# Operand loads of the down stage moved from GpSimd's queue to ScalarE's, one by one

## The chip, the core and the metric

The kernel runs on one NeuronCore of a Trainium2 chip. A core has five engines with a queue of instructions each: TensorE (PE in the profile; its weight loads are PEld), VectorE (DVE), ScalarE (ACT), GpSimd (POOL) and SyncE (SP). They work side by side and wait for each other by semaphores. Transfers between HBM and the on-chip memory are asked for by an instruction on SP's, ACT's or POOL's queue and carried by 16 DMA engines that all three share. The metric is the device time of one execution in microseconds.

## The reference

One encoder block over 512 positions of width 2048, all in float32. Attention, its output projection and the residual come first; this case is about the last part, the feed-forward network:

```python
h = rmsnorm(x, norm_ffn[l])
x = x + (jax.nn.silu(h @ w_gate[l]) * (h @ w_up[l])) @ w_down[l]
return rmsnorm(x, norm_final)
```

`w_gate` and `w_up` are 2048 x 5632, `w_down` is 5632 x 2048. The product with `w_down` is the down stage.

## The kernel before, in words

Every float32 operand is split into a high part and a low remainder (a CAST on ACT, then a subtraction on DVE), and each product is three matmuls: high x high, high x low, low x high (lines 184 to 186, the helper `mm3`). Matrix products of the feed-forward stages go by a Strassen-like scheme with seven products for a 2 x 2 block, named "11", "s3", "s2", "12", "s1", "22" and "s4"; the combinations of weights are made on DVE (L593, L596, L598, L603), then cast on ACT (L612) and subtracted on DVE (L613). Weights come through SP's queue (L583), four transfers of 512 KB for a unit.

In the gate and up stage (`unit_gu`, 44 units) each pair of hidden tiles leaves seven combinations, high and low side by side. They are written to HBM into `combos`, 1792 KB for a pair (7 x 512 floats, 14,336 bytes, in each of 128 partitions). The first pair and the last two do not take this way: their activations go as they are to `acts_kept`, stored by SP from the tile `raw` (L703).

The down stage starts with `unit_first`: four plain units for the first pair, whose results ACT copies out of PSUM (L768, L769) into eight accumulator tiles, one of them the former `raw`. Then come 19 pairs in five chunks of 4, 4, 4, 4 and 3 (`CHUNKS`). A chunk has four units (`unit_dn`, one for each quarter of the output's columns), and each unit runs the seven products over the chunk's pairs: 24 matmuls a product with four pairs. The results of a product lie in PSUM banks (of eight, handed out in turn) and are added to the accumulators (L790 of the kernel before; L806 and L814 copy a bank to a work tile on ACT, L810 forms the sum `u2` on DVE).

`load_operands` fetches a chunk's combinations from `combos`, one transfer for a pair (L747). Seven places take them in turn: `cp0` to `cp5` and `w0`, so pair i goes to place (i - 1) % 7, the next chunk's first three pairs have places that the running chunk does not use, and the fourth has to wait until PE leaves the running chunk's first place (for the later chunks, the previous one's). That fourth pair is asked for at the chunk's start; so the first unit of chunks 1 to 4 (`apart`) runs the first four products over three pairs, and then completes each with the fourth pair, by 6 matmuls (chunk 4 has no fourth pair). Before the change all 19 loads stand on POOL's queue: chunk 0's four in `unit_first`, the next chunk's first three in unit 1, the fourth in unit 0 of its own chunk.

PE's order is as written. The other engines' lists are put in order by the scheduler, from dependencies and its own estimate of when things are ready; so a request stands where the scheduler puts it, not where the source has it. Each engine runs its list strictly in that order.

Of the kernel before, what the change touches and what calls it, by code (L numbers as in the profile page):

```python
# [10 lines left out]
F32 = mybir.dt.float32  # L11
# [18 lines left out]
CHUNKS = [range(1 + 4 * c, min(5 + 4 * c, 20)) for c in range(5)]  # L30
# [15 lines left out]
def encoder_block(ctx: ExitStack, tc: tile.TileContext, io):  # L46
    nc = tc.nc
    pe, act, dve, pool = nc.tensor, nc.scalar, nc.vector, nc.gpsimd
# [23 lines left out]
    def bank():  # L72
        return psum.tile([P, 512], F32, name="bank")
# [7 lines left out]
    def w_tile():  # L81
        return work.tile([P, 512], F32, name="wk")
# [100 lines left out]
    def mm3(out, lh, ll, rh, rl, start, stop, **kw):  # L183
        pe.matmul(out, lh, rh, start=start, stop=False, **kw)  # L184
        pe.matmul(out, lh, rl, start=False, stop=False, **kw)  # L185
        pe.matmul(out, ll, rh, start=False, stop=stop, **kw)  # L186
# [382 lines left out]
    combos = tc.dram_tile((NF // 2, P, 7, 512), F32, name="combos")  # L569
# [50 lines left out]
    def product_of(i, j, ahead=3):  # L620
        make_to(i * 7 + j + ahead)
        return made[i * 7 + j]
# [97 lines left out]
    acts, acc, ops = {}, {}, {}  # L720
# [18 lines left out]
        for j, k in enumerate(((2, 1), (3, 0), (3, 1))):  # L739
            acc[k] = w[:, 2 * j:2 * j + 2].rearrange("p a q -> p (a q)")  # L740

    def load_operands(c, some=slice(None)):
        for i in CHUNKS[c][some]:
            n = (i - 1) % 7
            t = (pools["xa"], f"cp{n}") if n < 6 else (pools["mx"], "w0")
            ops[i] = t[0].tile([P, 7, 512], F32R, name=t[1])
            pool.dma_start(ops[i].bitcast(F32), combos[i])  # L747

    def unit_first():

        places_for_acc()
        load_operands(0)
        dve.tensor_scalar_mul(nr2, r2, -1.0)
        for u in range(DN):
            wh, wl = batch()
            if u == 3:
                limit[0] = len(UNITS) * 7
                make_to(NF * 7 + 2)
            b = [bank() for _ in range(NT)]
            for f in range(2):  # L760
                ws = slice(f * 512, (f + 1) * 512)
                for t in range(NT):
                    mm3(b[t], acts[f][:, t * P:(t + 1) * P], acts[f][:, 512 + t * P:512 + (t + 1) * P],
                        wh[:, ws], wl[:, ws], start=f == 0, stop=f == 1)
                yield
            for t in range(NT):
                o = acc[u, t // 2][:, (t % 2) * 512:(t % 2 + 1) * 512]
                act.copy(o[:, :256], b[t][:, :256])  # L768
                act.activation(o[:, 256:], b[t][:, 256:], AF.Copy, scale=-1.0)  # L769

    def unit_dn(c, u):
        pairs = CHUNKS[c]
        apart = c > 0 and u == 0
        if u == 0 and c > 0:
            load_operands(c, slice(3, None))
        if u == 1 and c + 1 < len(CHUNKS):
            load_operands(c + 1, slice(0, 3))
        i0 = NF + c * DN + u
        al, be, gm = bank(), bank(), bank()
        de = bank() if apart else al  # L780
        into = {"11": al, "s3": gm, "s2": de, "12": be, "s1": de, "22": gm, "s4": de}
        s1, u2 = w_tile(), w_tile()
        r = {(h, l): acc[u, l - 1].rearrange("p (t h q) -> p t h q", t=2, h=2)[:, :, h - 1]
             for h in (1, 2) for l in (1, 2)}

        def flat(x):
            return x.rearrange("p (t q) -> p t q", t=2)

        def add(h, l, x):
            dve.tensor_add(r[h, l], flat(x), r[h, l])  # L790

        def product(i, some):
            n = PRODUCTS[i]
            wh, wl = product_of(i0, i, 3 - i if some is early else 3)
            for p in some:
                x = ops[p][:, OPERAND[n]]
                ws = slice((p - pairs[0]) * 256, (p - pairs[0] + 1) * 256)
                for t in range(2):
                    mm3(into[n][:, t * 256:(t + 1) * 256], x[:, t * P:(t + 1) * P],
                        x[:, 256 + t * P:256 + (t + 1) * P], wh[:, ws], wl[:, ws],  # L800
                        start=p == pairs[0] and t == 0 and n in ("11", "s3", "12") + ("s2",) * apart,
                        stop=p == pairs[-1], skip_group_check=True)

        def after(i):
            if i == 0:
                act.copy(s1, al)  # L806
            elif i == 1:
                add(2, 2, gm)
            elif i == 2 and apart:
                dve.tensor_add(u2, de, s1)  # L810
                add(2, 2, s1)
                add(1, 2, s1)
            elif i == 2:
                act.copy(u2, al)  # L814
            elif i == 3:
                add(1, 1, be)
                add(1, 1, s1)
            elif i == 4:
                add(2, 2, de)
                add(2, 1, u2)  # L820
            elif i == 5:
                add(2, 1, gm)
            else:
                add(1, 2, de)

        early = pairs[:3]
        if apart:
            for i in range(4):
                product(i, early)
                yield  # L830
        for i in range(7):
            product(i, pairs[3:] if apart and i < 4 else pairs)
            after(i)
            if i0 == len(UNITS) - 1 and i == 3:
                prepare_last()
            yield
        if c == len(CHUNKS) - 1:
            for t in range(2):
                add_x1(t, u)

    def add_x1(t, u):
        x1 = w_tile()
        nc.sync.dma_start(x1, x1_kept[t, u])
        y = rest[t, u] = acc[u, t // 2][:, (t % 2) * 512:(t % 2 + 1) * 512]
        for h, r in enumerate((r2, nr2)):
            s = slice(h * 256, (h + 1) * 256)
            dve.scalar_tensor_tensor(y[:, s], y[:, s], r[:, t:t + 1], x1[:, s], op0=OP.mult, op1=OP.add)
# [16 lines left out]
    def prepare_last():  # L864
        for f in range(NF - CF, NF):
            act_tile(f, late_tile())
        load_gfin()
        fetch()
        fetch()
# [106 lines left out]
    for c in range(len(CHUNKS)):  # L976
        for u in range(DN):
            drive(unit_dn(c, u))
# [75 lines left out]
```

## Time and profile before

| | |
|---|---|
| median of 3 runs | 2224.97 us (2224.67 to 2231.49) |
| profiled execution | 2224.93 us, span 2223.2 us, granted TensorE clock 0.995 |
| busy share of PE, DVE, ACT, POOL | 98%, 75%, 45%, 0% |
| loads of `combos` on POOL's queue | 17 and 2, of 1792 KB |
| loads of weights on SP's queue (`st`) | 199 of 512 KB, 3.7 us to landing (median) |
| transfers on ACT's queue | 16 of 256 KB, all before the feed-forward stages |

The page of the profile has the busy time of each engine, the span in slices, the DMA queues, the chain of work that ended last, and the costliest groups of instructions. A row of the timeline has the start in us from the span's start, the length in us, engine, line, operation, output and inputs, and in brackets how long the engine stood idle before it and what ended that. A row of the waits has who waited, for whom, us in total, how often, and the longest. In a row for one tile, three numbers with slashes are the shortest, the median and the longest.

The down stage runs from about 1750 us: `unit_first` until 1772.5, chunk 0 until about 1852, chunks 1 to 4 until about 2160.

### The profile page before, as it was taken

How to read it: one execution, taken by the hardware profiler on the slowest of the kernel's cores; microseconds unless marked ns; L12 is line 12 of the kernel's file. 1: busy time of each engine (PE TensorE's matmuls, PEld its weight loads, DVE VectorE, ACT ScalarE, POOL GpSimd, SP SyncE). 2: the span in 40 equal slices, each digit the busy share in tenths (PEclk: the TensorE clock that was granted, in tenths of full speed). 3: DMA queues.
4: the chain of work that ended last, by engine and by line, in shares of the span. 5: the costliest groups of instructions: out<-in, count | busy, mean ns of one | idle time of the engine just before them, and what ended most of it. 6: DMA issues, size and time to landing. Idle time of an engine off the chain costs nothing. (4 is left out here: it accounts for less than half of the span.)

```text
span 2223.2 us, 37891 instructions
## 1 busy us (share of the span) xinstructions
PE 2187.6 (98%) x15754; PEld 2058.0 (93%) x15754; DVE 1661.5 (75%) x2373; ACT 1000.2 (45%) x1486; POOL 10.4 (0%) x23
## 2 busy tenths in 40 slices
PE   9999999999999999999999999999999999999997
PEld 8888888888888888999999999999999999999995
DVE  5655555676787447788888888888887498898897
ACT  6333333545555334444454444544444543343443
POOL 0000000000000000000000000000000000000000
PEclk9999999999999999999999999999999999999999
DMA  8222222222222453344454444544444746446344
GB/s 302 82 80 76 79 83 76 74 71 76 67 76 86 155 180 101 124 139 153 146 178 144 133 163 148 170 147 131 170 147 155 280 162 232 156 181 243 113 133 137
DMA packets 86908, 308.59 MB, mean 139 GB/s; under 512 B 10032, under 2 KB 11952, under 8 KB 84304
## 3 DMA queue, kind: packets, MB, share of 16 engines
q1 hardware_dynamic: 81696, 267.11, 36.8%
q0 software_dynamic: 2736, 34.87, 3.8%
q10 hardware_dynamic: 2304, 4.20, 0.5%
q8 instruction: 123, 2.02, 0.4%
q14 instruction: 49, 0.40, 0.1%
HBM read 261.31 MB, written 44.83 MB: 138 GB/s over the span
## 5 line engine op out<-in xcount | busy, mean ns | idle before, releaser
L612 ACT CAST hi<-m 128x1024 fp32r<-128x1024 f32 (+1 forms) x208 | 215.1, 1038 | 251.4 <-PE bank L185 124.4
L184 PE MATMUL bank<-cp,hi 128*128 128x256 f32 x1116 | 314.1, 281 | 0.1
L185 PE MATMUL bank<-cp,hi 128*128 128x256 f32 x1116 | 311.9, 280 | 0.0
L186 PE MATMUL bank<-cp,lo 128*128 128x256 f32 x1116 | 311.8, 279 | 0.0
L613 DVE TENSOR_TENSOR lo<-m,hi 128x1024 fp32r<-128x1024 f32 (+1 forms) x208 | 249.5, 1201 | 60.4 <-ACT hi L612 60.2
L121 DVE TENSOR_TENSOR lo<-st,hi 128x1024 fp32r<-128x1024 f32 (+1 forms) x136 | 165.0, 1214 | 142.6 <-ACT hi L120 138.9
L120 ACT CAST hi<-st 128x1024 fp32r<-128x1024 f32 (+1 forms) x136 | 141.7, 1042 | 194.9 <-PE bank L185 75.3
L185 PE MATMUL bank<-lo,cp 128*128 128x256 f32 (+1 forms) x738 | 209.0, 283 | 4.3 <-DVE lo L613 2.8
L184 PEld LDWEIGHTS bank<-cp,hi 128*128 128x128 f32 x1116 | 210.8, 189 | 0.5 <-ACT wk L665 0.3
L185 PEld LDWEIGHTS bank<-cp,hi 128*128 128x128 f32 x1116 | 210.3, 188 | 0.0
L186 PEld LDWEIGHTS bank<-cp,lo 128*128 128x128 f32 x1116 | 210.2, 188 | 0.0
L184 PE MATMUL bank<-hi,cp 128*128 128x256 f32 (+1 forms) x738 | 208.8, 283 | 0.7 <-DVE sums L790 0.7
L186 PE MATMUL bank<-hi,cp 128*128 128x256 f32 (+1 forms) x738 | 208.8, 283 | 0.0
L184 PE MATMUL bank<-xt,hi 128*128 128x512 f32 x512 | 206.3, 403 | 0.0
L184 PE MATMUL bank<-cp,m 128*128 128x256 f32 x732 | 205.4, 281 | 0.0
L185 PE MATMUL bank<-cp,m 128*128 128x256 f32 x732 | 204.2, 279 | 0.0
L186 PE MATMUL bank<-cp,m 128*128 128x256 f32 x732 | 204.2, 279 | 0.0
L186 PE MATMUL bank<-xt,lo 128*128 128x512 f32 x512 | 200.4, 391 | 0.0
L185 PE MATMUL bank<-xt,hi 128*128 128x512 f32 x512 | 199.9, 390 | 0.0
L612 ACT CAST m<-m 128x1024 fp32r<-128x1024 f32 (+1 forms) x112 | 116.8, 1043 | 144.2 <-PE bank L185 87.9
L613 DVE TENSOR_TENSOR m<-m,m 128x1024 fp32r<-128x1024 f32 (+1 forms) x112 | 135.3, 1208 | 39.1 <-ACT m L612 38.8
L185 PE MATMUL bank<-lo,xt 128*128 128x256 f32 x512 | 144.9, 283 | 0.7 <-DVE lo L121 0.6
(270 smaller groups left out, 5909.5 us busy)
## 6 DMA issues: line engine op xcount, KB each, us to landing
st<-w SPq DMA_DIRECT2D x199, 512.0 KB, 3.7
m<-w SPq DMA_DIRECT2D x180, 512.0 KB, 4.4
cp<-combos POOLq DMA_DIRECT2D x17, 1792.0 KB, 17.2
combos<-y SPq DMA_DIRECT2D x57, 512.0 KB, 4.5
combos<-y SPq DMA_DIRECT2D x19, 256.0 KB, 5.3
m<-w SPq DMA_DIRECT2D x12, 384.0 KB, 3.4
at<-x SPq DMA_DIRECT2D x8, 512.0 KB, 8.9
wk<-x SPq DMA_DIRECT2D x16, 256.0 KB, 5.3
```

Of the source, the lines that this page charges most:

```text
L120: act.copy(hi[:, s], st[:, s])
L121: dve.tensor_sub(lo[:, s], st[:, s], hi[:, s].bitcast(F32))
L184: pe.matmul(out, lh, rh, start=start, stop=False, **kw)
L185: pe.matmul(out, lh, rl, start=False, stop=False, **kw)
L186: pe.matmul(out, ll, rh, start=False, stop=stop, **kw)
L612: act.copy(hi[:, :n], w[name])
L613: dve.tensor_sub(lo[:, :n], w[name], hi[:, :n].bitcast(F32))
```

## The change

`load_operands` takes the queue as an argument. The next chunk's first three pairs are no longer asked for together in unit 1 on POOL's queue, but one each in units 1, 2 and 3, right behind the copy of the first product, on ACT's queue. Chunk 0's four loads and the fourth pair of chunks 1 to 3 stay on POOL's queue. It is 12 transfers that move.

```diff
-    def load_operands(c, some=slice(None)):
+    def load_operands(c, some=slice(None), queue=pool):
         for i in CHUNKS[c][some]:
             n = (i - 1) % 7
             t = (pools["xa"], f"cp{n}") if n < 6 else (pools["mx"], "w0")
             ops[i] = t[0].tile([P, 7, 512], F32R, name=t[1])
-            pool.dma_start(ops[i].bitcast(F32), combos[i])
+            queue.dma_start(ops[i].bitcast(F32), combos[i])
...
         if u == 0 and c > 0:
             load_operands(c, slice(3, None))
-        if u == 1 and c + 1 < len(CHUNKS):
-            load_operands(c + 1, slice(0, 3))
...
         def after(i):
             if i == 0:
                 act.copy(s1, al)
+                if u and c + 1 < len(CHUNKS):
+                    load_operands(c + 1, slice(u - 1, u), act)
```

What the scheduler makes of it shows at three places. ACT's list around the first units of the down stage, after the change (`hi` of L120 is a weight of `unit_first`, `y` an accumulator):

```order
L120 CAST hi<-st 128x1024 x2
L673 ACTIVATE wk<-wk 128x512
L747 DMA cp_18725<-combos 128x3584
L768 COPY y<-bank 128x256
L769 ACTIVATE y<-bank 128x256
...
L769 ACTIVATE y<-bank 128x256
L120 CAST hi<-st 128x1024 x2
L747 DMA cp_18950<-combos 128x3584
L768 COPY y<-bank 128x256
```

The requests for chunk 1's first two pairs stand in `unit_first`, ahead of its first and second four copies, and a cast that stood behind L673 before has moved behind the first four copies. In the same stretch the cast of the second product's weights, `hi<-st` of L612, has moved from ahead of the copies into `raw` to behind them and two more.

ACT's list at the start of chunk 1, after the change (`m`, `hi` and `st` hold weights; L804 is L806 of the kernel before):

```order
L612 CAST hi<-m_19138 128x1024
L747 DMA cp_19628<-combos 128x3584
L612 CAST hi<-m_19144 128x1024
L747 DMA cp_19853<-combos 128x3584
L804 COPY wk<-bank 128x512
L612 CAST m_19457<-st 128x1024
...
L612 CAST hi<-m_19366 128x1024
L747 DMA cp_20078<-combos 128x3584
```

The requests for chunk 2's first two pairs stand ahead of the copy of unit 0's first product, and the third four casts behind. The starts of chunks 2 and 3 read the same.

DVE's list at the same place, before:

```order
L603 TENSOR_TENSOR m_19140<-m_19140,m_19146 128x1024
L790 TENSOR_TENSOR y<-wk,y 128x2x256
L790 TENSOR_TENSOR y<-bank,y 128x2x256
L613 TENSOR_TENSOR m_19458<-st,m_19457 128x1024
L613 TENSOR_TENSOR lo<-m_19144,hi 128x1024
L810 TENSOR_TENSOR wk<-bank,wk 128x512
L790 TENSOR_TENSOR y<-wk,y 128x2x256
```

And after the change (L788 is L790 of the kernel before):

```order
L613 TENSOR_TENSOR lo<-m_19144,hi 128x1024
L788 TENSOR_TENSOR y<-bank,y 128x2x256
L810 TENSOR_TENSOR wk<-bank,wk 128x512
L788 TENSOR_TENSOR y<-wk,y 128x2x256
L613 TENSOR_TENSOR m_19458<-st,m_19457 128x1024
L613 TENSOR_TENSOR lo<-m_19142,hi 128x1024
```

L810 has moved ahead of the low parts of the fifth and sixth products' weights, and one addition from ahead of it to behind. In chunk 0's first unit, likewise, the low part `lo<-m` of the third product's weights (L613) has moved ahead of L593, which makes a combination for the next unit. SP's list and PE's are the same as before.

## The prediction

> **What bounds the kernel now.** The parts of the page come first: PE is busy for 98% of the span, so a change here pays only through PE's gaps. I therefore read the waits of PE alone over the down stage (1740 to 2120 us), with columns who waited, for whom, us in total, times, longest:
>
> ```profile
> PE 2187.6 (98%) x15754; PEld 2058.0 (93%) x15754; DVE 1661.5 (75%) x2373; ACT 1000.2 (45%) x1486; POOL 10.4 (0%) x23
> ...
> PE bank L184 <- DVE wk L810: 8.5, 3, 2.8
> PE bank L185 <- DVE lo L613: 2.8, 1, 2.8
> PE bank L184 <- DVE sums L790: 0.7, 1, 0.7
> ```
>
> That is all: 12.0 us in five gaps. None of them is a wait for an operand load, so the loads that the change moves are hidden today. What matters is what they do to their neighbours. First the list of DMA queues (packets, MB, share of the 16 DMA engines):
>
> ```profile
> q1 hardware_dynamic: 81696, 267.11, 36.8%
> q0 software_dynamic: 2736, 34.87, 3.8%
> q10 hardware_dynamic: 2304, 4.20, 0.5%
> ```
>
> q1 is SP's, q0 POOL's, q10 ScalarE's. POOL's 19 loads make 144 packets each: 128 rows of 14,336 bytes (34.87 MB / 2432) and one end mark for each of the 16 engines. So an engine gets 8 data packets per load, of 3.8% x 16 x 2223.2 / 2432 = 0.556 us each; a packet of SP's takes 36.8% x 16 x 2223.2 / 81696 = 0.16 us. ScalarE's queue has so far carried 16 small transfers of 144 packets, also one packet for a row (4.20 MB / 2048 = 2 KB). The next rows show the burst at the stage's start: POOL's seven loads with their shortest, median and longest time to landing, then the two small stores of SP that were asked for in the middle of it:
>
> ```profile
> L747 POOL DMA_DIRECT2D cp<-combos x6: 527/527/662, 1748.7 to 1752.1; - x6
> L747 POOL DMA_DIRECT2D w<-combos x1: 527/527/527, 1752.7 to 1752.7; - x1
> DMA to landing us min/median/max: 9.5/22.3/34.0
> ...
> L703 SPq DMA_DIRECT2D acts_kept<-raw x2: 652/930/1207, 1750.8 to 1751.6; - x2
>   ACT raw L768: 6.8, 1
> DMA to landing us min/median/max: 15.5/17.4/19.4
> ```
>
> The stores land at 1750.8 + 15.5 = 1766.3 and 1751.6 + 19.4 = 1771.0. The second is 8 packets of 1 KB per engine, and took 4.7 us behind the first: 0.58 us a packet, which is one POOL packet of 0.556 and its own short time. So **the queues take turns, packet by packet**: a queue with long packets makes every other queue wait one long packet per turn, and how much more stands in POOL's own queue matters to nobody else. The stores hold ScalarE (6.8 us), and nearly PE:
>
> ```profile
> 1770.99 0.37 ACT L768 COPY raw<-bank 128x256 f32<-128x256 f32 x1 [6.80 <-DMA acts_kept<-raw]
> 1771.26 0.39 ACT L769 ACTIVATE raw<-bank 128x256 f32<-128x256 f32 x1
> ...
> 1773.11 1.12 ACT L612 CAST hi<-m 128x1024 fp32r<-128x1024 f32 x1
> ...
> 1772.53 0.28 PE L184 MATMUL bank<-m,cp 128*128 128x256 f32 x1
> 1775.35 0.28 PE L184 MATMUL bank<-hi,cp 128*128 128x256 f32 x1
> ```
>
> The copy needs the tile `raw` back from the store and frees the PSUM bank (the eight rotate) into which chunk 0's first product goes. It ends at 1771.65 and PE enters at 1772.53: 0.9 us of slack.
>
> **The change, part by part.** POOL loses twelve loads and ScalarE gains twelve. The issue itself is cheap:
>
> ```profile
> 862.12 0.33 ACTq L493 DMA_DIRECT2D x_kept<-y  x1
> ```
>
> 12 x 0.33 = 4 us on an engine that is 45% busy; I cost it at nothing, and at 4 us if it stood on the path. The order of instructions, not the source, says where the requests go: ScalarE's list is reordered by readiness, and of each three the first two stand at the start of the running chunk's first unit, ahead of that unit's copy L804 (L806 before), not inside units 1 to 3. For chunk 1 they stand in `unit_first`, ahead of chunk 0. So they run together with POOL's own loads, on a second queue with rows as long.
>
> *Chunk 0.* On ScalarE's list the first request stands behind L673, and the second behind a cast that ran here at 1757:
>
> ```profile
> 1749.28 0.63 ACT L673 ACTIVATE wk<-wk 128x512 f32<-128x512 f32 x1 [0.25 <-DVE wk L672]
> ...
> 1756.95 1.05 ACT L120 CAST hi<-st 128x1024 fp32r<-128x1024 f32 x1
> ```
>
> So they go out at about 1750 and, with one more cast, 1759, while POOL's loads run. That is 16 long packets per engine. SP's second store needs 27 turns (8 packets and a mark for an operand tile and for each store), so all 16 get in front of it: 16 x 0.556 = 8.9 us, and the landing goes from 1771.0 to 1779.9. POOL's fourth load, the median one above, goes from 1773.0 to 1781.9 in the same way, when PE is just at its pair. After the slack of 0.9 the stall of chunk 0 is **+8.0 us**. Behind it the cast of the second product's weights comes later: it now stands behind four copies and their twins (1770.99 to 1773.11 is 2.1 us), the cast is 1 us and its low part 1.2, so low weights are there 4.4 us after the copy, while PE reaches them 0.9 + 2.82 (1772.53 to 1775.35) + 0.1 = 3.8 after: **+0.6**.
>
> Against that, one gap goes. DVE and PE at the third product:
>
> ```profile
> 1777.62 1.23 DVE L593 TENSOR_TENSOR st<-m,st 128x1024 f32<-128x1024 f32 x1 [9.78 <-issue]
> 1780.02 1.22 DVE L613 TENSOR_TENSOR lo<-m,hi 128x1024 fp32r<-128x1024 f32 x1
> ...
> 1781.29 0.38 PE L185 MATMUL bank<-lo,cp 128*128 128x256 f32 x1 [2.83 <-DVE lo L613]
> ```
>
> L593 stood idle until a weight load landed, with that low part behind it. The new order has the low part ahead of L593, and SP asks for the load earlier: **-2.8**. The next low part stays behind L593, due 9 us after the restart, with its load some 6 us behind the stores (8 turns of 0.7) and two operations of DVE to follow; I call it covered, just, and it costs some 2 us if it isn't. A stall of 8 us also costs clock. After shorter gaps two windows show (PE, PEld, DVE, ACT, POOL busy, granted clock, DMA):
>
> ```profile
> 1947.00:1952.00 5.00, 2.15 (x14) 1.98 (x14) 5.00 (x7) 2.85 (x4) 0.00 (x0) 0.88 1.00 426
> 1952.00:1956.00 4.00, 4.00 (x28) 4.00 (x28) 3.29 (x5) 0.96 (x1) 0.00 (x0) 0.72 0.99 416
> ```
>
> 5 x 0.12 + 4 x 0.28 = **+1.7** once more. Chunk 0 together: 8.0 + 0.6 - 2.8 + 1.7 = +7.5.
>
> *Starts of chunks 1 to 3.* POOL still asks for the fourth pair there, now in company. POOL's request, its landing, and PE's first matmul on the fourth pair:
>
> ```profile
> 1851.18 0.54 POOL L747 DMA_DIRECT2D cp<-combos  x1 [97.93 <-PE bank L186]
> DMA to landing us min/median/max: 7.9/7.9/7.9
> 1861.11 0.28 PE L184 MATMUL bank<-m,cp 128*128 128x256 f32 x1
> ...
> 1934.54 0.53 POOL L747 DMA_DIRECT2D cp<-combos  x1 [80.52 <-PE bank L186]
> DMA to landing us min/median/max: 7.8/7.8/7.8
> 1944.58 0.28 PE L184 MATMUL bank<-m,cp 128*128 128x256 f32 x1
> ...
> 2015.93 0.53 POOL L747 DMA_DIRECT2D cp<-combos  x1 [78.20 <-PE bank L186]
> DMA to landing us min/median/max: 8.6/8.6/8.6
> 2025.90 0.28 PE L184 MATMUL bank<-m,cp 128*128 128x256 f32 x1
> ```
>
> The slacks are 2.0, 2.2 and 1.4 us. ScalarE's first request waits for PE to leave the next pair's tile, 0.7 us behind POOL's; I take 7 of its 8 packets as getting in between, 7 x 0.556 = 3.9 (bounds: 0 if it starts late, 8 x 0.556 = 4.4). Stalls: 1.9 + 1.7 + 2.5 = **+6.1**. In front of ScalarE's next request is a cast, behind it the copy L804, which waits for PE until 1862 anyway.
>
> The three gaps of 2.8 us behind L810 stay, but shrink. Chunk 1's start on ScalarE and DVE:
>
> ```profile
> 1862.02 0.59 ACT L806 COPY wk<-bank 128x512 f32<-128x512 f32 x1 [8.08 <-PE bank L186]
> ...
> 1862.64 0.69 DVE L790 TENSOR_TENSOR y<-wk,y 128x512 f32<-128x512 f32 x1 [5.42 <-ACT wk L806]
> 1863.85 1.21 DVE L613 TENSOR_TENSOR m<-st,m 128x1024 fp32r<-128x1024 f32 x1
> 1866.12 0.68 DVE L810 TENSOR_TENSOR wk<-bank,wk 128x512 f32<-128x512 f32 x1
> ```
>
> PE waited for L810, behind two low parts. Now L810 stands ahead of them; PE then waits for the first low part: L810 can start at 1863.6, when the third short product is out (1861.11 + 3 x 0.71 + 0.3), and 0.6 + 0.6 + 1.2 behind it gives 1866.0 for 1866.8: -0.8, three times, **-2.4**. The weight loads of SP meet as many long packets as before, spread over two queues; I cost that at nothing, since the waits above show none for them past chunk 0.
>
> Sum: 7.5 + 6.1 - 2.4 = +11.2 us. The profiled execution took 2224.93 us (span 2223.2), the median of the runs is 2224.97: **2236 us**.
>
> **The rivals.** *ScalarE's packets are short.* No row shows one above 2 KB there, or above 4 KB on SP's queue, where the rows are no longer. With 4 KB of 0.16 us each the store loses 27 x 0.16 = 4.3 us, so chunk 0 costs 4.3 - 0.9 + 0.6 - 2.8 = +1.2, and 1.7 for the clock; the fourth pairs lose 8 x 0.16 = 1.3, under every slack; with -2.4 the change is +0.5, 2225.4. For it: nothing forbids it. Against: one packet for one row in all three queues. The Trainium skill, DMA: Bandwidth & Descriptors, section SWDGE vs HWDGE vs iDMA, has a packet as at most 4096 bytes "preferably"; by that this rival would hold, but the 14,336 bytes on q0 differ from it.
>
> *Faster.* ScalarE's loads start only when POOL's burst drains: then the store loses under 0.9 us, the gaps lose 2.8 and 2.4, and without the two slow windows of the clock after shorter gaps 3.4 more: -5.2 to -8.6, 2216 to 2220. For it: a load of SP's that was asked for in the burst took 11.3 us to land (KB each, us to landing), so a request can be slow to start:
>
> ```profile
> st<-w SPq DMA_DIRECT2D x1, 512.0 KB, 11.3
> ```
>
> Against: its 9 turns of 0.7 us are 6.4 of that, and 3.5 lie outside the packets even for POOL's load at 1851, alone: 7.9 less 8 x 0.556.
>
> *Worse.* Two gaps stand close together at each start, and the clock drops at all three for a second window, 3 x 1.7 more, with the 2 us of the later low part: 2241 to 2244. The Trainium skill, TensorE: Matmul & The Clock Gate, Part 1, has half clock after an idle window of about 3.4 us; by it gaps of 1.9 would cost nothing, but the trace shows 0.72 behind a gap of 2.8.
>
> *The change does what it says*: if the requests really went out one by one inside the units, the 6.1 would go: 2230.
>
> **How the numbers follow.** My forecast, between 2230 and 2241, 0.50; worse 0.14; short packets 0.22; faster 0.09; requests spread out 0.05. This kernel's measurement can tell 0.3%, 6.7 us, from no change: slower begins at 2231.7, faster ends at 2218.3. Slower takes most of the forecast and the worse case, 0.61; same the short packets, the spread requests and the forecast's low end, 0.32; faster 0.07. The range goes from 2222 to 2244; the forecast's own is 2230 to 2241.
>
> **What would show it.** In the profile after: ScalarE's queue with some 21.5 MB more and 14 KB packets; the copy L768 into `raw` held to about 1780 and PE's gap ahead of chunk 0's first product near 8 us; a gap of 1.5 to 2.5 us ahead of the fourth pair at three chunk starts, waiting for POOL's load; the gaps behind L810 gone over to a low part L613, near 2 us. Packets of 4 KB on ScalarE's queue, or stores that land by 1775, would make it wrong.

## The result

The change is slower by a little: 2231.27 us against 2226.13 us (medians of 20 runs each on one chip), a ratio of 1.0020 with an interval of 1.0012 to 1.0028. One of the 20 runs of the change took 4360.41 us, and the ratio leaves it out. A second comparison, of 12 runs with 28, gave 2232.64 against 2225.72, 1.0027 (1.0017 to 1.0037). So it costs 4.5 to 6 us by the ratios (5 to 7 by the medians), not the 11 of the forecast. The profiled execution took 2228.57 us, 3.6 more than the one before.

The page of the profile after, its lines on engines and queues:

```profile
PE 2187.4 (98%) x15754; PEld 2057.2 (92%) x15754; DVE 1661.7 (75%) x2373; ACT 999.8 (45%) x1486; POOL 4.0 (0%) x11
...
q1 hardware_dynamic: 81696, 267.11, 36.5%
q10 hardware_dynamic: 4032, 26.22, 2.9%
q0 software_dynamic: 1008, 12.85, 1.5%
```

ScalarE's queue, q10, has grown by 1,728 packets and 22.0 MB (the forecast said 21.5): twelve loads of 128 rows of 14,336 bytes with 16 end marks. The rival of short packets falls with this line. The waits of PE in the down stage (who waited, for whom, us in total, times, longest):

```profile
PE bank L184 <- ACT raw L769: 7.9, 1, 7.9
PE bank L185 <- DVE m L613: 3.9, 3, 1.3
PE bank L184 <- DMA cp<-combos: 3.8, 3, 1.5
PE bank L184 <- DVE wk L810: 0.8, 3, 0.3
```

Before there were 12.0 us of waits, now there are 16.4. The gap of 2.8 us at the third product and the one of 0.7 are gone. The three waits of 2.8 on L810 became 0.3 on L810 and 1.3 on the low part behind it, with a wait for the fourth pair ahead. The largest is new. ScalarE and PE at the end of `unit_first`, in the timeline, and the two stores that they wait for:

```profile
1778.62 0.37 ACT L768 COPY raw<-bank 128x256 f32<-128x256 f32 x1 [17.32 <-DMA acts_kept<-raw]
...
1779.33 0.58 PE L184 MATMUL bank<-m,cp 128*128 128x256 f32 x1 [7.85 <-ACT raw L769]
```

```profile
L703 SPq DMA_DIRECT2D acts_kept<-raw x2: 713/1020/1327, 1749.6 to 1750.4; - x2
  ACT raw L768: 17.3, 1
DMA to landing us min/median/max: 24.2/26.1/28.0
```

The second store lands at 1750.4 + 28.0 = 1778.4; it took 19.4 us before. Both traces have 15,754 matmul records, so the n-th can be set against the n-th. Up to the down stage the change is 1.2 us ahead (mainly half clock, a stretch in which TensorE's granted clock is 0.50, at 667 us, which only the trace before has). `unit_first`'s first matmul to chunk 0's first took 29.8 us, 21.8 before: +8.0. By the end of chunk 0, 6.6 us are lost. Chunks 1 to 3 give 0.4 back, and the last chunk and the end 1.3. That is 6.6 - 1.2 - 0.4 - 1.3 = 3.7, or 3.6 before rounding.

### The profile page after: what moved, and what is told of

Same layout as the page of the kernel before. It is cut to its first block, busy times and chain, and to the rows that moved or that the text cites. A ratio compares the mean times of both kernels' runs of the same rounds, so it can differ in the third digit from the quotient of the medians.

```text
span 2226.8 us, 37853 instructions
## 1 busy us (share of the span) xinstructions
PE 2187.4 (98%) x15754; PEld 2057.2 (92%) x15754; DVE 1661.7 (75%) x2373; ACT 999.8 (45%) x1486; POOL 4.0 (0%) x11
## 4 chain that ended last, share of the span: by engine, by line
issue 47%; PE 45%; DVE 4%; DMA 3%; ACT 1%; SPq 0%; ACTq 0%; POOLq 0%; POOL 0%; DVEq 0%
PE bank L184 14%; PE bank L185 14%; PE bank L186 14%; PE bank L303 1%; DMA cp<-combos 1%; DMA st<-w 1%; PE bank L403 1%; PE bank L404 1%; DVE lo L613 0%; DMA combos<-y 0%; DVE m L613 0%; PE bank L428 0%; PE bank L533 0%; DMA wk<-x_kept 0%; DVE w L544 0%
## 5 line engine op out<-in xcount | busy, mean ns | idle before, releaser
L612 ACT CAST hi<-m 128x1024 fp32r<-128x1024 f32 (+1 forms) x208 | 215.3, 1038 | 248.5 <-PE bank L185 122.7
L613 DVE TENSOR_TENSOR lo<-m,hi 128x1024 fp32r<-128x1024 f32 (+1 forms) x208 | 249.7, 1201 | 59.4 <-ACT hi L612 59.1
L120 ACT CAST hi<-st 128x1024 fp32r<-128x1024 f32 (+1 forms) x136 | 141.7, 1042 | 194.7 <-PE bank L185 74.7
L612 ACT CAST m<-m 128x1024 fp32r<-128x1024 f32 (+1 forms) x112 | 116.8, 1043 | 141.8 <-PE bank L185 86.3
L613 DVE TENSOR_TENSOR m<-m,m 128x1024 fp32r<-128x1024 f32 (+1 forms) x112 | 135.3, 1208 | 38.5 <-ACT m L612 38.4
## 6 DMA issues: line engine op xcount, KB each, us to landing
cp<-combos ACTq DMA_DIRECT2D x10, 1792.0 KB, 12.8
```

The costliest lines, as they stand in the source:

```text
L120: act.copy(hi[:, s], st[:, s])
L612: act.copy(hi[:, :n], w[name])
L613: dve.tensor_sub(lo[:, :n], w[name], hi[:, :n].bitcast(F32))
```

## The experiments

Each ran against the kernel before on the same chip; ratios are to that kernel, with a 95% interval. For e7, e3 and e12 the interval leaves out 1 only by 0.0001 or 0.0002.

| | median us | before | ratio |
|---|---|---|---|
| e14 the change again | 2232.64 | 2225.72 | 1.0027 (1.0017 to 1.0037) |
| e1 only chunk 1's loads undone | 2235.81 | 2228.00 | 1.0036 (1.0022 to 1.0050) |
| e9 only chunk 1's loads changed | 2232.51 | 2226.38 | 1.0027 (1.0017 to 1.0037) |
| e7 `raw` used last | 2229.61 | 2228.00 | 1.0011 (1.0001 to 1.0022) |
| e5 rows of 2 KB | 2232.67 | 2228.00 | 1.0020 (1.0010 to 1.0030) |
| e6 fourth pair on ScalarE's queue | 2225.90 | 2226.38 | 0.9994 (0.9984 to 1.0004) |
| e11 copies without the hold | 2230.64 | 2226.38 | 1.0019 (1.0009 to 1.0028) |
| e3 requests held | 2224.48 | 2228.00 | 0.9988 (0.9978 to 0.9999) |
| e12 order only | 2222.96 | 2225.72 | 0.9988 (0.9978 to 0.9998) |
| e8 held, and the order | 2218.88 | 2226.38 | 0.9967 (0.9954 to 0.9980) |
| e13 the same from POOL's queue | 2218.14 | 2225.72 | 0.9970 (0.9959 to 0.9981) |

### The change in two halves (e1, e9), and once more (e14)

e1, against the change:

```diff
+        if u == 1 and c == 0:
+            load_operands(1, slice(0, 3))
...
-                if u and c + 1 < len(CHUNKS):
+                if u and c and c + 1 < len(CHUNKS):
                     load_operands(c + 1, slice(u - 1, u), act)
```

> Only chunk 1's three loads go back to POOL's queue, all at once in unit 1 of chunk 0, as before the change; those of chunks 2 to 4 stay on ScalarE's queue. So the start of chunk 0 is as before (7.85 us of TensorE's wait on the eviction into raw gone, the 2.83 us gap at the third product back), and what is left against the kernel before is what the starts of chunks 1 to 3 do. The forecast's step (1.9+1.7+2.5 of fourth-pair stalls less 2.4 of the waits on the L810 copy = +3.7): 3.7 us over the kernel before, about 2229.8. The reading of the trace of the change (stalls of 0.84, 1.42 and 1.50, together 3.8, in place of 8.5 less 4.7 = 3.8 of the waits on VectorE): within 1 us of the kernel before, 2225 to 2227, or up to 1.4 us below it if the end of the program, too, is quicker for a reason that lies in the later chunks.

It was 7.8 us over the kernel before (4.9 to 11 by the interval): both expectations were too low, and half of the change costs more than the whole. PE's waits, and POOL's three fourth pairs with their landing (e1, then the change):

```profile
PE bank L184 <- DMA cp<-combos: 8.1, 3, 3.1
PE bank L185 <- DVE m L613: 3.9, 3, 1.3
PE bank L185 <- DVE lo L613: 3.2, 1, 3.2
...
L747 POOL DMA_DIRECT2D cp<-combos x3: 530/530/539, 1853.3 to 2023.8; - x3
DMA to landing us min/median/max: 12.2/12.9/13.3
```

```profile
L747 POOL DMA_DIRECT2D cp<-combos x3: 527/527/527, 1856.5 to 2021.3; - x3
DMA to landing us min/median/max: 11.0/11.7/11.7
```

The fourth pair lands 1.2 to 1.6 us later than in the change, and its waits are 2.1, 3.1 and 2.8. The packets in the traces say where the difference begins. After POOL's request, POOL's first packet starts 1.2 us later in every run. ScalarE's first starts 2.1 us later in e1, but 3.1 to 3.5 in the change, e14 and e7 (one of e11's at 5.0: that pair landed after 9.5 us; another at 2.5: 12.1 us). The earlier ScalarE's packets begin, the more of them lie between POOL's. ScalarE's request itself comes 0.30 us behind POOL's in e1, and 0.42 in the change. Why its first packet then takes 1.8 us in one and 2.7 in the other isn't settled; with no other transfer under way, at e6's fourth pairs, it took 0.96.

The other part of e1's loss is the clock that TensorE was granted. Stretches of e1 and of the change (PE, PEld, DVE, ACT, POOL busy, granted clock, DMA share, GB/s):

```profile
1950.80:1954.20 3.40, 0.83 (x7) 0.83 (x8) 0.00 (x0) 0.00 (x0) 0.00 (x0) 1.00 1.02 433
1954.20:1957.60 3.40, 3.40 (x19) 3.40 (x18) 1.33 (x3) 3.14 (x4) 0.00 (x0) 0.50 0.64 269
```

```profile
1869.90:1873.30 3.40, 1.85 (x14) 1.48 (x13) 3.35 (x4) 2.99 (x4) 0.00 (x0) 1.00 1.04 429
1873.30:1876.70 3.40, 3.40 (x18) 3.40 (x18) 3.40 (x5) 0.00 (x0) 0.00 (x0) 0.50 0.98 413
```

A stretch of 3.4 us in which PE stood much is followed by one at half clock: 18 or 19 matmuls touch it in place of some 31, so about 1.5 us are lost. If half of PE's time at half clock counts as lost, which is a little too much by this, the clock cost e1 12.8 us (2.8 of them in chunk 0), and the kernel before 8.5. So e1's waits are 4.0 us longer (16.0 to 12.0) and its clock loses some 4.3 more: about 8.3 of the 9.7 us by which its profiled execution is longer.

e9 is the other half:

```diff
+        if u == 1 and 0 < c < len(CHUNKS) - 1:
+            load_operands(c + 1, slice(0, 3))
...
-                if u and c + 1 < len(CHUNKS):
+                if u and c == 0:
                     load_operands(c + 1, slice(u - 1, u), act)
```

> The other half of e1: only chunk 1's three loads come one by one from ScalarE's queue as in the change; those of chunks 2 to 4 go back to POOL's queue, three at once in unit 1, as before. What is over the kernel before is then the price of chunk 0 alone. If the parts simply add (chunk 0's ledger in the trace of the change: 6.8 at its start, 5.4 over it), 5.4 to 7.5 us over the kernel before, more than the whole change. If instead the clock's half steps carry much of e1's 8 us (its trace has 17.4 us lost to the clock against 12.6 of the kernel before), the sum of the two halves has no fixed size, and this one lands anywhere from 3.5 to 9 us over, by how many of the waits at the chunk starts are followed by half a clock.

6.1 us over the kernel before (3.8 to 8.2): chunk 0 alone costs as much as the whole change. PE waits 7.4 us at its start, and at the starts of chunks 1 to 3 the 8.5 us on the sum of L810 (here L812) are back:

```profile
PE bank L184 <- DVE wk L812: 8.5, 3, 2.8
PE bank L184 <- ACT raw L769: 7.4, 1, 7.4
```

By this difference, what the change does at chunks 1 to 3 comes to about nothing, while e1 alone paid 7.8 us there. The halves give 14 us in sum, the whole 4.5 to 6, so the parts can't be added: each half has its own waits, by when ScalarE's packets begin, and its own half clocks.

> The change as it is, a second time. If the waits follow from the program, they come back: 7 to 8 us at the start of chunk 0, 0.8 to 1.5 on the fourth pair of chunks 1 to 3, 1.29 on the part for product 4 three times; 1.0012 to 1.0028 of the kernel before. What may differ are the stretches of half clock: each wait of 1.3 to 2.9 us is followed by one or not.

```profile
PE bank L184 <- ACT raw L769: 8.0, 1, 8.0
PE bank L184 <- DMA cp<-combos: 3.9, 3, 1.6
```

These waits and the two others come back to within 0.2 us in sum, but this profiled execution took 2231.98 us, 3.4 more than the first of the same kernel. The difference is the clock: counted as for e1, half clock cost 10.9 us here, 7.7 in the first. Spans less that loss are 2219.3 and 2219.1, and 2214.7 for the kernel before. At full clock the change costs about 4.5 us, twice.

### What the start of chunk 0 waits for (e7)

```diff
-        acc[2, 0] = pools["mk"].tile([P, 1024], F32, name="raw")
+        acc[3, 1] = pools["mk"].tile([P, 1024], F32, name="raw")
...
-        for j, k in enumerate(((2, 1), (3, 0), (3, 1))):
+        for j, k in enumerate(((2, 0), (2, 1), (3, 0))):
```

> The buffer raw, which unit_first's third unit evicts into (acc[2,0]), serves as the last accumulator (acc[3,1]) instead; the three others move up. Loads are those of the change. Theory A, that the start of chunk 0 waits for the store out of raw alone (landed at 1778.44): evictions that don't need raw go on, TensorE reaches chunk 0 some 7 us earlier and stops nowhere for long: 7 us under the change, about 2224. Theory B, that POOL's late fourth load (landed at 1781.25) would hold TensorE almost as long: the wait moves to the fourth pair of chunk 0's first product, a wait on a load of combos of 5 to 6 us that ends at about 1781, and only 1.5 to 2.5 us are gained: 2229 to 2230. I hold B for the likelier.

The store still lands late (27.5 us), but nothing of PE's stands behind it now. PE instead waits for chunk 0's third and fourth pairs, POOL's own loads (the change's, with their landing, and e7's PE):

```profile
L747 POOL DMA_DIRECT2D cp<-combos x4: 528/530/662, 1747.5 to 1749.5; - x4
DMA to landing us min/median/max: 14.7/25.3/31.7
```

```profile
1774.98 0.39 PE L184 MATMUL bank<-m,cp 128*128 128x256 f32 x1 [2.35 <-DMA cp<-combos]
1780.15 0.58 PE L184 MATMUL bank<-m,cp 128*128 128x256 f32 x1 [3.97 <-DMA cp<-combos]
```

6.3 us of the 7.85 stay, and the time is that of theory B. The store was only the wait that ended last; all that stands in the other two queues is late by the same packets.

### Turns between the queues (e5, e6)

```diff
             if queue is act:
+                for n in range(7):
+                    act.dma_start(ops[i][:, n].bitcast(F32), combos[i][:, n])
```

> Each of the twelve loads on ScalarE's queue is asked for as seven transfers with rows of 2,048 bytes in place of one with rows of 14,336; bytes, places and queue as in the change. If the transfer engines take turns between queues packet by packet (the forecast's way: 16 packets of 0.556 us ahead of the store at the start of chunk 0, 7 ahead of the fourth pair), a packet of a seventh of the bytes, some 0.08 us, holds the others up by a seventh: about 36 turns x 0.08 = 2.9 us instead of 8.9 at the start of chunk 0, the wait there 2 to 3 us instead of 7.85, and 0.6 instead of 3.9 at the fourth pairs, whose waits are gone: 7 to 9 us under the change, 2222 to 2225. If they share by bytes, the packet's size tells nothing: the wait of 7.85 stays, and the time is that of the change, 2230 to 2232.

The landings are as turns by packet have them. POOL's loads in e5, at the starts of chunks 1 to 3 and in `unit_first`:

```profile
L751 POOL DMA_DIRECT2D cp<-combos x3: 530/530/530, 1851.5 to 2019.1; - x3
DMA to landing us min/median/max: 8.4/8.5/9.2
...
L751 POOL DMA_DIRECT2D cp<-combos x4: 530/530/664, 1745.7 to 1747.7; - x4
DMA to landing us min/median/max: 11.2/18.6/26.1
```

8.4 to 9.2 us against 11.0 to 11.7, though 23 to 32 of ScalarE's packets per engine lay between them, 8 to 9 in the change; the slowest in `unit_first` took 26.1 against 31.7. But the time was that of the change, so my expectation of 2222 to 2225 failed. At chunk 0's start PE still waited 5.2 us (3.1 and 2.1), not the 2 to 3 expected, and at the later starts something else stood in the way. ScalarE's timeline says what:

```profile
1853.38 12.13 ACTq L749 DMA_DIRECT2D cp<-combos  x11
1865.56 0.59 ACT L808 COPY wk<-bank 128x512 f32<-128x512 f32 x1 [11.14 <-DMA cp<-combos]
```

Of the 14 requests of a chunk's start only seven went out at once; from the eighth on each waited until an earlier transfer had landed, and the copy and the casts stood behind them. PE waited 9.6 us for those casts, which this edit and not the packets caused.

e6 asks for the fourth pair from ScalarE's queue as well, ahead of the other three:

```diff
-            load_operands(c, slice(3, None))
+            load_operands(c, slice(3, None), act)
```

> The change, and the fourth pair of chunks 1 to 3 asked for from ScalarE's queue too, ahead of the three that follow; POOL's queue has only chunk 0's four. Theory of turns between queues: with one queue the fourth pair is not shared with anything and lands in 7.5 to 9 us, ahead of TensorE (which comes to it 10.2 us after the request); the waits of 0.84, 1.42 and 1.50 are gone, the wait of 7.85 at the start of chunk 0 stays: 3.8 us under the change, 2226 to 2228. Rival, that the delay lies in what all transfers of a chunk's start share (the memory's rate or the engines'), whichever queue asks: waits of 0.8 to 1.5 stay, 2230 to 2232.

```profile
PE bank L184 <- ACT raw L769: 8.0, 1, 8.0
PE bank L185 <- DVE m L613: 2.1, 3, 0.7
PE bank L184 <- DVE wk L810: 2.0, 3, 0.7
```

With nothing ahead of it in its queue and no long packets beside it, the fourth pair landed after 7.7, 7.7 and 8.0 us, and no wait for it is left: 2225.9, just below the 2226 to 2228 expected. The wait at chunk 0 stays. Turns between queues with long packets are the cause of the fourth-pair waits. The Trainium skill, DMA: Bandwidth & Descriptors, Queues, rings and completion order, has each DMA engine go round its queues a packet at a time; e5's and e6's landings agree.

### The time of the request, or the queue (e3, e11, e13)

In e3 a copy of one column from the unit's own `s1` stands ahead of each of the twelve requests; the load overwrites the column.

```diff
+            if queue is act:
+                act.copy(ops[i][:, 0, :1], s)
             queue.dma_start(ops[i].bitcast(F32), combos[i])
...
-                    load_operands(c + 1, slice(u - 1, u), act)
+                    load_operands(c + 1, slice(u - 1, u), act, s1[:, :1])
```

> The same twelve loads on ScalarE's queue, but each behind a copy of one column from the unit's own s1 into the tile that it fills, so that a request can't leave before product 0 of units 1, 2 and 3 has ended (the load overwrites the column, so the result is the same). Theory A, that the loss comes from requests that leave early (1748.65 and 1755.36, between POOL's four; 1856.88 and 1858.37, behind the fourth pair of chunk 1) and share the transfer engines with what is needed at once: the 7.85 us wait at the start of chunk 0 and the three waits on the fourth pair (0.84, 1.42, 1.50) are gone, the fourth pair lands in under 9 us, and the 2.83 us gap at the third product of chunk 0 does not return; the waits on the L810 copy return to about 2.8 each. Sum against the kernel before: -2.8 for that gap, up to -1.6 for the 0.74 gap and the half clock around it: 2222 to 2224, 7 to 9 us under the change. Theory B, that the wait at the start of chunk 0 comes from POOL's own four loads and the stores, whatever ScalarE's queue asks: the 7.85 us stay, and the time is 2227 to 2231.

ScalarE's timeline in chunk 0's second unit, and PE's waits in the whole stage:

```profile
1795.19 0.19 ACT L748 CAST cp<-wk 128x1 fp32r<-128x1 f32 x1
1795.41 0.33 ACTq L749 DMA_DIRECT2D cp<-combos  x1
```

```profile
PE bank L184 <- DVE wk L812: 8.5, 3, 2.8
```

Now the requests do leave one by one, at 1795, 1815 and 1835, and theory A holds: only the 8.5 us on L812 are left of the waits, the fourth pairs land after 7.6 to 8.3 us, and the gap at the third product does not return. 2224.48 is 3.5 us under the kernel before, a little above the 2222 to 2224 expected.

e11 has the same copies, from a tile that is ready early (`nr2` in place of `s1`):

> A control for e3: the same one-column copy ahead of each of the twelve requests, but from a tile that is ready from the start of the down stage, so the request is not held back until its unit. If what e3 gained is the time of the request, this one loses as the change does: a wait of 7 to 8 us at the start of chunk 0, fourth pairs that land after 10 to 12 us, 2229 to 2232. If the copy itself did it (a changed order on ScalarE, a tile written ahead of the load), it is as e3, 2223 to 2225. The copy puts ScalarE's first request at the starts of chunks 1 to 3 some 0.3 to 0.5 us later behind POOL's than in the change (0.42 us), so fewer of its packets should lie ahead of the fourth pair: landing near 10.5 us instead of 11.0 to 11.7.

```profile
PE bank L184 <- ACT raw L771: 7.3, 1, 7.3
PE bank L185 <- DVE m L613: 3.8, 3, 1.3
PE bank L184 <- DMA cp<-combos: 3.4, 2, 2.2
```

2230.64: it loses as the change does, so the copy is not what helps. The request did not come later as I had thought (0.41 to 0.67 us behind POOL's), and landings spread from 9.5 to 12.1 us.

e13 is e8 (below) with the held requests on POOL's queue, `pool.tensor_copy` and `pool.dma_start` in place of ScalarE's:

> As e8, but the three held requests of a chunk come from POOL's queue, each behind POOL's own copy of one column. If the time of the request is what counts and not the queue, it is as e8: no wait on a load at any chunk's start, no gap in chunk 0, 2217 to 2221. If ScalarE's queue has a worth of its own (its loads landed in 8.3 to 9.7 us in e3, none of them waited for), POOL's would show waits on loads that e8 has not, or VectorE and POOL would hold each other up: 2222 to 2226.

0.9970 beside e8's 0.9967, and the same waits to a tenth. With the requests held, these runs show no difference between the two queues. What counts is what else is under way. The kernel before asks for the next chunk's pairs as early as the change does (at chunk 1's start from 1852.0 to 1853.5 us), but on POOL's queue, behind the urgent pair's request at 1851.2, and that pair landed after 7.9 us.

### The order at a chunk's start (e12, e8)

```diff
-            wh, wl = product_of(i0, i, 3 - i if some is early else 3)
+            wh, wl = product_of(i0, i, 3 - i if some is early or apart and i < 3 else 3)
```

> The kernel before, all loads from POOL's queue as there, and only the order that e8 adds: product 2's sum ahead of the parts for products 4 and 5 at a chunk's first unit. Theory, that e8's gain is the sum of two things that have nothing to do with each other: the three waits of 2.85 fall to 0.58 plus 1.29 as in e8, 1.0 each, and no half clock follows them (up to 3.4 us in two of three starts): 3 to 5 us under the kernel before, 2221 to 2224 beside 2226 to 2228; the 2.83 us gap in chunk 0 stays. Rival, that the order pays only where the fourth pair is early and the queues are free: within 1.5 us of the kernel before.

e12, on the kernel before, and then e8, on e3:

```profile
PE bank L185 <- DVE m L613: 3.9, 3, 1.3
PE bank L185 <- DVE lo L613: 2.7, 1, 2.7
PE bank L184 <- DVE wk L810: 1.7, 3, 0.6
```

> The held requests of e3 and one thing more: at a chunk's first unit the parts for products 4 and 5 are made only after product 2's sum (the copy of line 810) and no longer ahead of it, so VectorE comes to that sum two operations of 1.2 us earlier; the change had this order on VectorE, the kernel before and e3 did not. Theory: the three waits of 2.845 us on that sum fall to about 0.3 plus 1.3 on the part for product 4, as in the trace of the change, 1.3 each, 3.9 in all, and a wait of under 1.5 us halves the clock after it less often than one of 2.8 (which cost e3 1.7 us at two of its three starts): 4 to 6 us under e3, 2218 to 2221. Rival: the parts made later are missed at products 4 and 5, and waits of 1.3 to 2.5 us there take the place of the gain: 2223 to 2226.

```profile
PE bank L185 <- DVE m L613: 3.9, 3, 1.3
PE bank L184 <- DVE wk L812: 1.7, 3, 0.6
```

The order alone gains 2.8 us, a little less than I expected (3 to 5), and one stretch of half clock at a chunk's start stayed, at 1950.6 us. The hold alone gains 3.5; together they gain 7.5, and 2218.88 is the best of all these kernels with e13. In e8 no stretch of half clock is left in the down stage: 5.6 us of waits, none over 1.3.

## Why the prediction was wrong

**Right: the way it loses at chunk 0.** The list of instructions was read rightly, that ScalarE's first two requests leave during `unit_first`; so were the long packets and the turns. The stall was +8.0 against +8.0 forecast, the store landed at 1778.4 for 1779.9, POOL's fourth load at 1781.2 for 1781.9, and the gap of 2.8 went. (The trace after is 1.2 us ahead here, so on the clock of the one before they are 1779.6 and 1782.4.) e7 and e9 bear this out. Chunk 0 as a whole cost 6.6 for 7.5, and that it came so near is partly luck. The clock took 2.4 us there, not 1.7; the +0.6 for the second product's weights shows in no wait; and some 0.9 us came back because the matmuls ran at the faster of their two paces (last section) from 1785 on, in the trace before only from 1793.

**The step that failed: starts of chunks 1 to 3, "+6.1" and "-2.4".** The mechanism was right (e6: one queue, no wait), both sizes were off, and to the same side. The fourth pairs' stalls were 0.84 + 1.42 + 1.50 = 3.8. I took 3.9 us of delay each; two of the three were 3.1 (11.0 - 7.9 and 11.7 - 8.6). And PE came to the pair some 0.3 us later after POOL's request than before, which I took as fixed. Behind the sum of L810 the saving was 1.3 at each start (2.85 to 0.27 + 1.29), not 0.8, and so 3.8 in all. Most likely the wait for the fourth pair had already let VectorE and ScalarE catch up: in e8, without that wait, the saving is 1.0. So 3.8 of waits came and 3.8 went: nothing, for +3.7 forecast. e1 shows how weak a fixed "7 packets" is: there the same three stalls came to 8.1.

**Left out.** The gap of 0.74 at 1893, for which the sum had no term, went away with its restart (0.9 us). And I priced the clock only at chunk 0. Two of the three old 2.8 us waits were each followed by half a clock; in the first profile of the change one of the three shorter ones was, in e14 all three. That is 1.5 us less in the one and 1.5 more in the other, which no sum of mean costs could tell. PE's start behind a wait had no term either: some 0.2 us each, nine waits in place of four, 1.0 in all. With these terms, and 0.9 us for slightly slower matmuls in the first profile (117.5 ns against 117.0), chunks 1 to 3 come to -0.4 us there and to +2.0 in e14. Outside the down stage's first four chunks the first trace after gained 2.5 us (1.2 ahead of them, 1.3 behind), where the forecast had nothing.

**The base.** 2224.93 was one execution; later medians of the same kernel were 2225.7 to 2228.0. Set against these, a forecast by differences would have been 1 to 3 us higher still.

**The rivals.** Short packets fell with the page after. *Faster* fell with the trace after: ScalarE's packets began at 1752.2 us, and POOL's ran until 1780.1. *Worse* (2241 to 2244) had half clock at all three starts: e14 shows that, yet at 2231.98, as its stalls were smaller. *Requests spread out inside the units* did not happen in the change; e3 made it happen, and it gained 3.5 us, where I had priced it at 2230: I took away only the 6.1 of the fourth pairs and left the 7.5 of chunk 0, though requests inside units 1 to 3 would have spared chunk 0 too. That was a slip of mine.

## What to carry to other kernels

Where a source line asks for a transfer says nothing about when the request leaves: if its destination is free, it leaves as soon as the engine's list comes to it, and only a dependency on the work it is meant to follow (here a one-column copy) holds it back. A second queue did not speed up the transfer that was urgent; long rows on it took their turn between the urgent ones (landing after 11.0 to 11.7 us in place of 7.8 to 8.6), so ask for prefetches when nothing urgent is in flight, or in one queue behind it. And a wait has two prices, its length and what the clock does after it; look at both before a stall is worth removing.

## What the runs showed of the hardware

**The clock goes by fixed windows.** In each of these traces half clock begins and ends on one grid of 3.413 us: in the kernel before at 667.4, 879.0, 1950.8 and 2032.7 us, which are 62, 314 and 24 steps apart. What a wait costs depends on where it falls. Two waits of 2.84 us in the kernel before, one over two windows, one within one:

```profile
1862.00:1865.40 3.40, 2.10 (x18) 1.89 (x17) 2.76 (x4) 3.38 (x5) 0.00 (x0) 1.00 1.01 420
1865.40:1868.80 3.40, 1.86 (x16) 1.89 (x17) 3.40 (x5) 0.98 (x2) 0.00 (x0) 1.00 0.99 419
1868.80:1872.20 3.40, 3.40 (x31) 3.40 (x31) 3.40 (x6) 1.05 (x1) 0.00 (x0) 1.00 1.03 431
1947.40:1950.80 3.40, 0.55 (x5) 0.42 (x4) 3.40 (x5) 2.45 (x3) 0.00 (x0) 1.00 1.01 431
1950.80:1954.20 3.40, 3.40 (x18) 3.40 (x18) 3.40 (x5) 0.00 (x0) 0.00 (x0) 0.50 0.98 416
```

With PE busy for 0.55 of 3.40 us the next window has half the clock, with 2.10 and 1.86 it has not; 1.85 was followed by half in the change (above). Over all windows at full clock in the 13 traces, on the exact grid, PE busy for under 1.45 us was always followed by half clock (48 windows) and for over 1.92 us never; between the two, half clock followed in 14 of 32. So the border lies near half of the window, and in that band the busy time alone doesn't decide. The Trainium skill, TensorE: Matmul & The Clock Gate, Part 1, has a free-running window of 3413 ns, which agrees, and half clock after an idle window, which does not: windows more than half busy were enough here.

**Matmuls come at two paces at full clock.** The same shapes, 128x256, in 45 us of chunk 0 of the kernel before, and of e13:

```profile
1800.00:1845.00 45.00, 45.00 (x399) 45.00 (x399) 40.25 (x43) 19.59 (x22) 0.00 (x0) 1.00 0.40 129
```

```profile
1800.00:1845.00 45.00, 45.00 (x384) 45.00 (x384) 39.87 (x42) 19.03 (x21) 3.17 (x4) 1.00 0.58 225
```

That is 113 ns against 117 each, both with PE busy throughout and the clock at 1.00. The faster pace comes in stretches of up to 74 us in chunks 0 and 2 (61 and 63 us in the kernel before, none in e12 and e13, at most 17 us in the other chunks). Over the 125 us it is worth some 4 to 5 us, about as much as the whole change. It is not the DMA load alone (the kernel before has the slower pace in chunk 1 with a DMA share of 0.36). I found no cause, and no run was made for it. It can't explain the loss: the change's two traces have more of the faster pace than the kernel before (138 and 142 us against 125). But e8's profiled 2214.24 us, 3.6 under e13's 2217.80 with the same waits, goes with 153 us of the faster pace in e8's execution and none in e13's. So part of a difference between single executions can be this pace. How it varies from execution to execution of one kernel isn't shown, and so it isn't shown either that medians as close as those of e3, e7 and e12 to the kernel before are free of it.
